# A two-layer hybrid encoder: pair rows of 288 columns, operands at multiples of 256 bytes

## The chip, the core and the metric

The kernel runs on one core of one Trainium2 chip. The metric is the device time of one execution in microseconds. A core has TensorE (PE, the matrix engine, with a sequence of weight loads, PEld, beside the matmuls), VectorE (DVE), ScalarE (ACT), GpSimd (POOL) and SyncE (SP, which here issues the transfers from the main memory HBM). Data lies in SBUF, 128 partitions with a byte address within the partition; TensorE writes its sums to PSUM, 8 banks of 512 float32 per partition. All engines run beside each other and wait for each other by semaphores.

## The reference, cut to what matters

Two layers of an encoder over 16 meta tokens and 256 tokens (272 in all) of width 2048:

```python
for l in range(2):
    proj = h @ w_in[l]                      # 2048 -> 6176 columns
    gq, gk, gv, gr, glr, nq, nk, nv = split(proj)
    y_gla = gated_linear_attention(gq, gk, gv, gr, glr)    # both directions
    y_na = neighbourhood_attention(nq, nk, nv)
    mix = concat(y_gla, y_na) @ w_out[l]    # 2048 -> 2048
    h = layer_norm(ALPHA * h + mix)
    ff = square(relu(h @ w_ff1[l])) @ w_ff2[l]             # 2048 -> 8192 -> 2048
    h = layer_norm(ALPHA * h + ff)
return h[:, 16:]
```

All of it is float32. The weights of the four dense products are some 400 MB; each is read once.

## The kernel before, in words

**Float32 from pairs.** A float32 matmul is made of faster ones on a reduced type (`F32R`). Every operand is split into a high part, the value rounded to `F32R`, and a low part, the value minus the high part (`split`, L262: a ScalarE copy for the high part and a VectorE subtraction for the low one). A product is then high times high, high times low and low times high.

**Pairs of activations.** The activations are held transposed: a *pair* (L41, made by `pair`, L272) holds 128 of the 2048 columns, one per partition, and in each partition two rows: the high part of all tokens and, behind it, the low part. There are 16 x pairs (the normed input of a layer or of its MLP), 16 y pairs (the concatenated attention outputs, later the first 16 chunks of the MLP's inner activations), and for the MLP 16 u pairs more (its other inner chunks; L786). An x pair's rows are 274 float32 wide, because two more columns hold a layer norm's gain and bias; y and u rows are 272 wide. The sums over partitions that the layer norms and the GLA heads need (`mean`, L871, matmuls at L878) go through pairs named `sp`. Pools place tiles one behind the other, each rounded up to 32 bytes; constants come first (L74), then x pairs (pool `xhl`), y pairs (`yhl`), and the weight tiles (`wst`).

**Weight tiles.** `order` (L145) yields all weights in the order of their use in tiles of 128 partitions x 1024 float32. `made` (L167) loads a tile to `raw` by SyncE's queue, copies it to `wh` on ScalarE (L175) and makes `wl` on VectorE (L176). Each of the three names has three buffers; two tiles are kept ready ahead of TensorE (L161).

**The dense products.** `by_m` (L245) makes 128 output columns at a time: for each weight tile, `eight` (L199) multiplies 8 chunks of 128 x 128 weights with 8 pairs. In layer 0, with 272 tokens, L211 does 16 matmuls of 272 columns per tile (`wh` chunk j with the high row, then with the low row of pair j) and L214 does 8 (`wl` chunk j with the high row). In layer 1 only the 256 tokens count (`once`): L208 does 8 matmuls of 512 columns, which read 256 columns of the high row and 256 of the low row of a pair in one instruction, and L214 does 8 of 256 columns. Where a product needs the gain and bias columns too, there are 274 or 258 columns. `by_k` (L225, matmuls at L241) runs over the input chunks in the outer loop, where the input becomes ready chunk by chunk; its matmuls have the same operands.

**Order of the work.** TensorE's queue is strict: tiles of dense products, and between them, by credits (`pump`, L116), steps of generators for the GLA heads, the neighbourhood attention and the layer norms. The order is fixed when the program is built. Names in the profile: `mm<-x,wh` is a matmul with a moving row of an x pair and a stationary chunk of `wh`.

Other tiles take the places of pairs that are not in use: `load_gates` (L369) puts gate weights in y pairs, `reuse` (L936) puts output rows and the last layer norm's rows in x pairs; both take 512 columns of the two rows seen as one.

Of the kernel before, what the change touches and what calls it, by code (L numbers as in the profile page):

```python
# [7 lines left out]
F32 = mybir.dt.float32  # L8
F32R = mybir.dt.float32r
# [5 lines left out]
P = 128  # L15
# [4 lines left out]
L = T + NM  # L20
# [15 lines left out]
LEAD = 4  # L36
WARM = 14
MEET = 2


class Pair(tuple):  # L41
# [8 lines left out]
class Trunk:  # L50
# [23 lines left out]
    def consts(self):  # L74
        nc, c = self.nc, self.cp
        t = lambda n, s, d=F32: c.tile(s, d, name=n, tag=n)
        self.vec = t("vec", [P, DEPTH, 66])
        nc.sync.dma_start(self.vec, self.i["vec"].rearrange("l p v -> p l v"))
        self.ident = t("ident", [P, P])
        nc.sync.dma_start(self.ident, self.i["ident"])  # L80
        self.sel = t("sel", [LRK, 2])
        nc.sync.dma_start(self.sel, self.i["sel"])
        self.qmask = t("qmask", [NM, NK2])
        nc.sync.dma_start(self.qmask, self.i["qmask"])
        self.mask = t("mask", [P, 5, 32], U8)
        raw = self.wp.tile([P, WB], F32, name="raw", tag="raw")[:, :5 * 32].rearrange("p (l c) -> p l c", l=5)
        nc.sync.dma_start(raw, self.i["mask"])
        nc.gpsimd.tensor_copy(self.mask, raw)
        self.ones = {}
        for n in (GDV, 4 * P, D):  # L90
            self.ones[n] = t(f"ones{n}", [P, P])
            nc.gpsimd.memset(self.ones[n], 1.0 / n)
        self.ones_r = {}
        for n in self.ones:
            self.ones_r[n] = t(f"onesr{n}", [P, P], F32R)
            nc.scalar.copy(self.ones_r[n], self.ones[n])
        self.eps = t("eps", [P, 1])
        nc.gpsimd.memset(self.eps, EPS)
        self.one = t("one", [P, 1])
        nc.gpsimd.memset(self.one, 1.0)  # L100
# [15 lines left out]
    def pump(self, fg, bg, meet=False):  # L116
# [10 lines left out]
        while self.credit >= 1:  # L127
            if self.bg and self.wants.get(self.bg[0]):
                alone = meet and not some
                if ran or alone and self.late < MEET:  # L130
                    self.late += alone and not ran
# [138 lines left out]
        self.nc.vector.tensor_tensor(dst[low:low + n], src, dst[high[0]:high[0] + n].bitcast(F32), ALU.subtract)  # L270

    def pair(self, pool, name, c):  # L272
        w = L + 2 if name == "x" else L
        return Pair(pool.tile([P, 2, w], F32R, name=f"{name}{c}", tag=f"{name}{c}", bufs=1))


    def layer(self, l):
# [90 lines left out]

    def load_gates(self):  # L369

        place = lambda c: self.yp.tile([P, 2, L], F32, name=f"gw{c}", tag=f"y{c}", bufs=1).rearrange("p a c -> p (a c)")[:, :512]
        *self.wup, self.wlr = (place(c) for c in (8, 9, 10))
        for d, w in enumerate(self.wup):
            self.nc.sync.dma_start(w[:LRK], self.i["wup"][self.l, :, d])
        self.nc.sync.dma_start(self.wlr, self.i["wlr"][self.l])
# [559 lines left out]

    def reuse(self, name, c, dtype):  # L936

        t = self.xp.tile([P, 2, L + 2], dtype, name=f"{name}{c}", tag=f"x{c}", bufs=1)
        return t.rearrange("p a c -> p (a c)")[:, :512]

    def affine(self, l, which, k):
# [231 lines left out]
```

## Time and profile before

| what | value |
|---|---|
| time, median of 3 runs | 2379.57 us (2379.57 to 2380.83) |
| span of the profiled execution, first to last instruction | 2377.1 us |
| mean granted TensorE clock | 0.999 |
| instructions in the profile | 44606 |
| HBM read, mean rate | 414.03 MB, 175 GB/s |

The profile gives the span of its execution; the time of a run is taken outside the core and is longer by what lies around the span, here 2.5 us between the median and the profiled span.

How to read it. The page has numbered parts: busy time of each engine; the span in 40 slices; the DMA queues; the chain of work that ended last, followed back from the last instruction; groups of instructions; transfers. A group's row reads: line, engine, operation, output<-inputs by the program's names, shape, count, then busy us and mean ns of one, then idle time before them. Matmuls are pipelined, so the mean of one (some 290 ns) is far longer than the distance from one to the next. In the timeline, equal instructions in a row are merged: start in us, length in us, engine, line, operation, count. The distance between the starts of two such rows is the time that the engine took from the one to the other.

### The profile page before, as it was taken

The numbers are of one execution on the slowest core, as the hardware profiler recorded it, in microseconds if no ns is written. First come the engines' busy times: TensorE is split into PE (matmuls) and PEld (weight loads), VectorE is DVE, ScalarE is ACT, GpSimd is POOL, SyncE is SP. The second block draws the span as 40 slices with busy tenths as digits, with TensorE's granted clock in tenths as the row PEclk, the third lists the DMA queues.
The fourth block names the chain that finished last, engine by engine and source line by source line (L and its number), as shares of the span: only waits on it lengthen the run. The fifth ranks groups of instructions, "written<-read, shape, count | busy, mean of one in ns | idle before, by whom it ended". The sixth has DMA issues, their size and how long they took to land.

```text
span 2377.1 us, 44606 instructions
## 1 busy us (share of the span) xinstructions
PE 2368.7 (100%) x18180; PEld 2249.8 (95%) x18180; DVE 1520.7 (64%) x2432; ACT 1221.2 (51%) x2100; POOL 135.2 (6%) x200
## 2 busy tenths in 40 slices
PE   9999999999999999999999999999999999999998
PEld 9999999999999999999999899999988888888888
DVE  5588777775544455546576787778766455666654
ACT  5666664564433344444456667655644333444443
POOL 0011100100000000000021111000100000000000
PEclk9999999999999999999999999999999999999999
DMA  8455445555555555565555555556666666666664
GB/s 261 152 159 152 148 138 171 174 173 175 177 177 177 174 175 178 171 176 176 175 186 163 168 164 154 161 154 192 193 189 186 187 189 190 188 187 206 199 192 143
DMA packets 118301, 419.02 MB, mean 176 GB/s; under 512 B 13512, under 2 KB 14024, under 8 KB 118096
## 3 DMA queue, kind: packets, MB, share of 16 engines
q1 hardware_dynamic: 117808, 415.65, 57.9%
q8 instruction: 142, 2.33, 0.4%
q14 instruction: 63, 0.52, 0.1%
q10 hardware_dynamic: 288, 0.52, 0.1%
HBM read 414.03 MB, written 2.10 MB: 175 GB/s over the span
## 4 chain that ended last, share of the span: by engine, by line
PE 98%; DVE 1%; issue 0%; ACT 0%; POOL 0%; DVEq 0%; ACTq 0%; POOLq 0%
PE mm L211 36%; PE mm L214 29%; PE mm L208 22%; PE mm L241 6%; PE bg L241 1%; PE bg L752 1%; PE mm L691 1%; PE bg L552 0%; PE bg L398 0%; DVE wl L176 0%; PE mm L717 0%; PE mm L441 0%; PE bg L878 0%; PE bg L603 0%; PE bg L633 0%
## 5 line engine op out<-in xcount | busy, mean ns | idle before, releaser
L176 DVE TENSOR_TENSOR wl<-raw,wh 128x1024 fp32r<-128x1024 f32 (+1 forms) x768 | 941.5, 1227 | 633.7 <-ACT wh L175 625.0
L175 ACT CAST wh<-raw 128x1024 fp32r<-128x1024 f32 (+1 forms) x768 | 804.1, 1048 | 932.7 <-PE mm L211 432.6
L211 PE MATMUL mm<-x,wh 128*128 128x272 f32 (+2 forms) x4224 | 577.8, 289 | 0.0
L211 PEld LDWEIGHTS mm<-x,wh 128*128 128x128 f32 x4224 | 548.5, 189 | 0.8 <-PE mm L691 0.2
L214 PE MATMUL mm<-x,wl 128*128 128x272 f32 (+3 forms) x3264 | 467.3, 285 | 0.0
L214 PEld LDWEIGHTS mm<-x,wl 128*128 128x128 f32 x3264 | 437.6, 188 | 13.2
L208 PE MATMUL mm<-x,wh 128*128 128x512 f32 x1152 | 293.7, 397 | 0.0
L208 PEld LDWEIGHTS mm<-x,wh 128*128 128x128 f32 x1152 | 207.7, 189 | 39.4 <-PE mm L691 0.4
L214 PE MATMUL mm<-y,wl 128*128 128x272 f32 (+1 forms) x1408 | 199.0, 284 | 0.0
L211 PE MATMUL mm<-y,wh 128*128 128x272 f32 (+1 forms) x1440 | 195.2, 287 | 0.0
L214 PEld LDWEIGHTS mm<-y,wl 128*128 128x128 f32 x1408 | 188.1, 188 | 7.4
L211 PEld LDWEIGHTS mm<-y,wh 128*128 128x128 f32 x1440 | 185.9, 188 | 0.0
L208 PE MATMUL mm<-y,wh 128*128 128x512 f32 x688 | 172.6, 392 | 0.0
L214 PE MATMUL mm<-u,wl 128*128 128x272 f32 (+1 forms) x1024 | 144.5, 283 | 0.0
L208 PEld LDWEIGHTS mm<-y,wh 128*128 128x128 f32 x688 | 123.1, 188 | 21.2
L211 PE MATMUL mm<-u,wh 128*128 128x272 f32 (+1 forms) x1056 | 142.6, 287 | 0.0
L214 PEld LDWEIGHTS mm<-u,wl 128*128 128x128 f32 x1024 | 136.6, 188 | 5.6
L211 PEld LDWEIGHTS mm<-u,wh 128*128 128x128 f32 x1056 | 135.9, 188 | 0.0
L208 PE MATMUL mm<-u,wh 128*128 128x512 f32 x496 | 125.3, 395 | 0.0
L208 PEld LDWEIGHTS mm<-u,wh 128*128 128x128 f32 x496 | 89.1, 188 | 16.4
L241 PE MATMUL mm<-x,wh 128*128 128x272 f32 (+1 forms) x512 | 73.1, 287 | 0.0
L241 PEld LDWEIGHTS mm<-x,wh 128*128 128x128 f32 x512 | 67.5, 189 | 0.0
(273 smaller groups left out, 1853.6 us busy)
## 6 DMA issues: line engine op xcount, KB each, us to landing
raw<-in_wff SPq DMA_DIRECT2D x512, 512.0 KB, 3.6
raw<-in_win SPq DMA_DIRECT2D x190, 512.0 KB, 4.0
raw<-in_wout SPq DMA_DIRECT2D x64, 512.0 KB, 3.7
nb<-in_nab SPq DMA_DIRECT2D x16, 352.0 KB, 4.8
xraw<-in_xT SPq DMA_DIRECT2D x7, 272.0 KB, 6.3
out<-out SPq DMA_DIRECT2D x5, 256.0 KB, 3.2
brow<-in_norm SPq DMA_DIRECT2D x4, 256.0 KB, 5.5
gw<-in_wup SPq DMA_DIRECT2D x4, 196.0 KB
```

The costliest lines, as they stand in the source:

```text
L175: nc.scalar.copy(wh[:, c], raw[:, c])
L176: self.wl = nc.vector.tensor_tensor(wl[:, c], raw[:, c], wh[:, c].bitcast(F32), ALU.subtract).ins
L208: mm(ps, lhsT=c(wh, j), rhs=v.both[:, :, :T], start=first and not j, stop=False)
L211: mm(ps[:, :n], lhsT=c(wh, j), rhs=v[i][:, :n], start=first and not i + j, stop=False)
L214: mm(o, lhsT=c(wl, j), rhs=h[:, :T if once else n], start=False, stop=last and j == 7)
L241: self.nc.tensor.matmul(ps[g + m][:, :n], lhsT=parts[p][0][:, c:c + P], rhs=acts[k + j][parts[p][1]][:, :n], start=k + j + p == 0, stop=k ...
L691: nc.tensor.matmul(ps[hh][:, t * NKEY:t * NKEY + NKEY], lhsT=q[hs, NM + t * P:NM + t * P + P], rhs=k[hs, t, :], start=True, stop=True)
L752: nc.tensor.matmul(po[t][hs, :P], lhsT=v2[ts, hs] if rest else v1[:, t, hs], rhs=p2[ts, hh, :] if rest else p1[:, 2 * hh + t, :], start=re ...
```

## The change

Rows of every pair become 288 float32 wide (1,152 bytes), so that a pair takes 2,304 bytes, nine times 256. A tile of 40 float32 per partition, which nothing reads or writes, goes ahead of the constants and moves all that follows. By the built program's addresses, x pairs then begin at byte 13,056, y pairs at 49,920, `raw`, `wh` and `wl` at 86,784, 99,072 and 111,360, u pairs at 124,672, all at multiples of 256; a pair's low row begins 1,152 bytes behind its high row. Before, x pairs began at byte 21,088 and stood 2,208 bytes apart, y pairs began at 56,416 and u pairs at 129,120, both 2,176 apart, and the weight tiles began at 91,232, 103,520 and 115,808. The wider rows take more space; the constructor's reserve for software-made DMA descriptors at the start of SBUF is halved from 16,384 to 8,192 bytes. The places that reuse pairs follow the new width. What the instructions read, compute and write is the same.

```diff
+PAD = 40
+PITCH = 288
...
     def consts(self):
         nc, c = self.nc, self.cp
         t = lambda n, s, d=F32: c.tile(s, d, name=n, tag=n)
+        t("pad", [P, PAD])
         self.vec = t("vec", [P, DEPTH, 66])
...
     def pair(self, pool, name, c):
-        w = L + 2 if name == "x" else L
-        return Pair(pool.tile([P, 2, w], F32R, name=f"{name}{c}", tag=f"{name}{c}", bufs=1))
+        return Pair(pool.tile([P, 2, PITCH], F32R, name=f"{name}{c}", tag=f"{name}{c}", bufs=1))
...
     def load_gates(self):
-        place = lambda c: self.yp.tile([P, 2, L], F32, name=f"gw{c}", tag=f"y{c}", bufs=1).rearrange("p a c -> p (a c)")[:, :512]
+        place = lambda c: self.yp.tile([P, 2, PITCH], F32, name=f"gw{c}", tag=f"y{c}", bufs=1).rearrange("p a c -> p (a c)")[:, :512]
...
     def reuse(self, name, c, dtype):
-        t = self.xp.tile([P, 2, L + 2], dtype, name=f"{name}{c}", tag=f"x{c}", bufs=1)
+        t = self.xp.tile([P, 2, PITCH], dtype, name=f"{name}{c}", tag=f"x{c}", bufs=1)
...
-    nc = bacc.Bacc("TRN2", target_bir_lowering=False, num_devices=1)
+    nc = bacc.Bacc("TRN2", target_bir_lowering=False, num_devices=1, dynamic_dma_scratch_size=8192)
```

## The prediction

> **What bounds the kernel now.** I read the page's parts 1, 3 and 4 first, to see which engine sets the end.
>
> ```profile
> PE 2368.7 (100%) x18180; PEld 2249.8 (95%) x18180; DVE 1520.7 (64%) x2432; ACT 1221.2 (51%) x2100; POOL 135.2 (6%) x200
> ...
> q1 hardware_dynamic: 117808, 415.65, 57.9%
> ...
> PE 98%; DVE 1%; issue 0%; ACT 0%; POOL 0%; DVEq 0%; ACTq 0%; POOLq 0%
> PE mm L211 36%; PE mm L214 29%; PE mm L208 22%; PE mm L241 6%; PE bg L241 1%; PE bg L752 1%; PE mm L691 1%; PE bg L552 0%; PE bg L398 0%; DVE wl L176 0%; PE mm L717 0%; PE mm L441 0%; PE bg L878 0%; PE bg L603 0%; PE bg L633 0%
> ```
>
> TensorE is busy for the whole span and makes up 98% of the chain that ended last; 93% of the chain are the four lines of the dense matmuls (L211, L214, L208, L241). Transfers take 57.9% of the DMA engines, VectorE is at 64%: neither is late for anything. So the change is worth what it does to the time of one matmul, times some 16,000.
>
> That time is best read from the timeline of TensorE, where the matmuls of one weight tile stand as one row and the distance of two starts is the time of a whole tile. Before the change, in layer 0, on the x pairs (start us, us, line, operation):
>
> ```profile
> 603.64 2.18 PE L211 MATMUL mm<-x,wh 128*128 128x272 f32 x16
> ...
> 606.66 2.18 PE L211 MATMUL mm<-x,wh 128*128 128x272 f32 x16
> ...
> 609.69 2.18 PE L211 MATMUL mm<-x,wh 128*128 128x272 f32 x16
> ```
>
> Two tiles of 24 matmuls (16 of L211, 8 of L214) take 609.69 - 603.64 = 6.05 us: 3.025 each, 126 ns per matmul. The same view on the y and u pairs, whose matmuls have the same shape and count:
>
> ```profile
> 798.51 2.18 PE L211 MATMUL mm<-y,wh 128*128 128x272 f32 x16
> ...
> 801.52 2.15 PE L211 MATMUL mm<-y,wh 128*128 128x272 f32 x16
> ...
> 804.50 2.16 PE L211 MATMUL mm<-u,wh 128*128 128x272 f32 x16
> ...
> 807.49 2.16 PE L211 MATMUL mm<-u,wh 128*128 128x272 f32 x16
> ...
> 810.47 2.18 PE L211 MATMUL mm<-y,wh 128*128 128x272 f32 x16
> ```
>
> 3.01, 2.98, 2.99 and 2.98 us, on average 11.96 / 4 = 2.99. Nothing but the place of the operands in the memory differs between these tiles and the x tiles, so **place does cost something**: 0.035 us per tile (1.2%) between x and y or u, and 0.03 between two halves of y. In layer 1, where L208 reads both rows of a pair in one matmul of 512 columns:
>
> ```profile
> 1271.99 2.03 PE L208 MATMUL mm<-x,wh 128*128 128x512 f32 x8
> ...
> 1274.80 2.03 PE L208 MATMUL mm<-x,wh 128*128 128x512 f32 x8
> ...
> 1277.60 0.54 PE L398 MATMUL bg<-x,ws 128*64 128x272 f32 x3
> ```
>
> ```profile
> 1960.08 2.00 PE L208 MATMUL mm<-y,wh 128*128 128x512 f32 x8
> ...
> 1962.85 2.01 PE L208 MATMUL mm<-y,wh 128*128 128x512 f32 x8
> ...
> 1965.64 2.02 PE L208 MATMUL mm<-u,wh 128*128 128x512 f32 x8
> ...
> 1968.45 2.02 PE L208 MATMUL mm<-u,wh 128*128 128x512 f32 x8
> ```
>
> x takes 5.61 / 2 = 2.805 us per tile, y 2.77 and 2.79, u 2.81: (1968.45 - 1960.08) / 3 = 2.79 on average.
>
> What part of a tile could a better place save? The last tiles of the program have the shape of layer 0 with 256 columns:
>
> ```profile
> 2358.19 2.05 PE L211 MATMUL mm<-u,wh 128*128 128x256 f32 x16
> ...
> 2361.02 2.05 PE L211 MATMUL mm<-u,wh 128*128 128x256 f32 x16
> ```
>
> 2.83 us against u's 2.985 with 272 columns: 16 columns cost 0.155 us / 24 = 6.5 ns, 0.40 ns a column. At that rate 272 columns are 110 ns, and some 15 of the 125 ns of a matmul do not grow with its columns. Only those can go.
>
> **The change part by part.** *Instructions.* None is added or removed. On TensorE, ScalarE, VectorE and SyncE the built programs have the same instructions in the same order with the same waits; one semaphore signal at the end of layer 0's last L214 tiles comes one matmul earlier, because a memset of GpSimd then overlaps u28 where it overlapped u29. No wait is new, nothing is queued behind anything else. The smaller scratch in the constructor is reserved memory for descriptors that no transfer of this kernel uses (the queues of part 3 are hardware queues): 0.
>
> *Addresses.* The tiles' sizes and the pools' order give them, and the built program lists them. Before, x pairs stand 2,208 bytes apart from byte 21,088 on and their low row begins 1,096 bytes after the high one: high rows begin at a multiple of 64 for odd chunks and 32 past one for even chunks, low rows 8 past a multiple of 32. y and u pairs stand 2,176 bytes apart, both rows always 32 past a multiple of 64. Weight tiles begin 96 past a multiple of 256. After, every high row and every weight tile begins at a multiple of 256, every low row 128 past one.
>
> *What that does to x.* The x tiles are the only ones with rows of several kinds of start, and they take longest in layer 0. After the change they have one kind, as y and u have had. The nearest price is y's and u's own level: x goes from 3.025 to 2.99. The number of such tiles, from the groups by form:
>
> ```profile
> L211 PE MATMUL mm<-x,wh 128*128 128x272 f32 x3584 | 491.1, 289 | 0.0
> L208 PE MATMUL mm<-x,wh 128*128 128x512 f32 x1152 | 293.7, 397 | 0.0
> ...
> L211 PE MATMUL mm<-y,wh 128*128 128x272 f32 x1408 | 191.2, 287 | 0.0
> L208 PE MATMUL mm<-y,wh 128*128 128x512 f32 x688 | 172.6, 392 | 0.0
> ...
> L211 PE MATMUL mm<-u,wh 128*128 128x272 f32 x1024 | 138.5, 287 | 0.0
> L208 PE MATMUL mm<-u,wh 128*128 128x512 f32 x496 | 125.3, 395 | 0.0
> ```
>
> 3584 / 16 = 224 tiles: -224 x 0.035 = **-7.8 us**. In layer 1, 1152 / 8 = 144 tiles from 2.805 to 2.79: -144 x 0.015 = **-2.2 us**. Other forms on x, of 274 and 258 columns and by L241:
>
> ```profile
> L211 PE MATMUL mm<-x,wh 128*128 128x272 f32 (+2 forms) x4224 | 577.8, 289 | 0.0
> ...
> L241 PE MATMUL mm<-x,wh 128*128 128x272 f32 (+1 forms) x512 | 73.1, 287 | 0.0
> ```
>
> are (4224 - 3584) / 16 + 512 / 16 = 72 tiles, at the same 0.035: **-2.5 us**.
>
> [...]
>
> *What that does to y and u.* They had one kind of start (32 past a multiple of 64) and get another. The bounds come from their own spread, 2.98 to 3.01, and x's 3.025; their mean is the value I take: 0. The 88 + 64 tiles of layer 0 may move by -0.01 to +0.035 each (-1.5 to +5.3 us), the 86 + 62 of layer 1 from -0.02 to +0.015 (-3.0 to +2.2).
>
> *Is a start at a multiple of 64 worth more in itself?* The trace has one place where rows begin there one after the other: the sums of the layer norms (L878) in layer 1, on the sp pairs; in layer 0 the same matmuls begin 32 past such a multiple.
>
> ```profile
> 1650.10 0.52 PE L878 MATMUL bg<-sp,onesr 128*128 128x256 f32 x3
> 1650.46 0.52 PE L211 MATMUL mm<-x,wh 128*128 128x258 f32 x3
> ```
>
> ```profile
> 454.38 0.66 PE L878 MATMUL bg<-sp,onesr 128*128 128x272 f32 x4
> 454.88 0.29 PE L211 MATMUL mm<-x,wh 128*128 128x274 f32 x1
> ```
>
> 0.36 / 3 = 120 ns with 256 columns aligned, 0.50 / 4 = 125 with 272 not aligned; less 16 columns of 0.40 that is 118.5. Aligned rows are no faster there. That their weights stood 32 past a multiple of 64 is what this does not answer.
>
> *Transfers, copies, splits.* Weight rows now land at a multiple of 256, and ScalarE and VectorE read and write other addresses: 57.9%, 51% and 64% busy beside a full TensorE, so even 10% more or less on them would not reach the end. What hides them is TensorE's own work; without that cover a change of 10% on VectorE, the busier of the two, would be some 150 us of its 1520.7.
>
> *Sum.* -7.8 - 2.2 - 2.5 = -12.5 us on a span of 2377.1, so 2364.6. The runs' median is 2379.57, 2.5 us over the profiled span, and I add those: **2367 us**.
>
> **The rivals.**
>
> *Place makes no difference on the whole* (chance 0.20): a long or a short tile is a matter of which row meets which weight chunk, and a new layout reshuffles them with the same mean. For it: y's halves, with equal kinds of rows, differ by 0.03. Time: 2379.6, within 4.8 us.
>
> *Collision, slower* (chance 0.30): rows and weight chunks begin in the same class of addresses after the change, in each of the matmuls, where before only some did. If TensorE's two streams, moving rows and the next weights, get in each other's way when they start in the same class, each tile pays what now only some pay. For it: x against y, and y's halves, show that pairing has a price. Against it: the sp rows, and that y's even rows start in the weights' class (96 past a multiple of 256) without standing out as a whole tile. Price: y and u go to x's level, 152 x 0.035 + 148 x 0.015 = +7.5 us; if x too goes up by one more such step, (152 + 224 + 72) x 0.035 + 144 x 0.015 = +17.8 more. 2387 to 2405, I take 2392. It decides as soon as a tile in layer 0 takes over 3.02 on average. [...]
>
> *A whole block is saved per row* (chance 0.12): if rows are fetched in blocks of 64 bytes, a row that begins 32 past a multiple touches one block more than an aligned one, 16 columns or 6.5 ns. For it: 15 ns per matmul don't grow with the columns, and no trace here has aligned rows together with aligned weights. Against it: the sp rows, and x, whose odd high rows are aligned already (8 of a tile's 24 rows) and which is no faster. Price: y and u 24 rows, x 16 rows: (152 + 148) x 24 x 6.5 ns = 47 us, (224 + 144 + 72) x 16 x 6.5 ns = 46 us; 93 in all, 2287. [...]
>
> **How the numbers follow.** The forecast has a chance of 0.38 (own range 2355 to 2374), no difference 0.20, collision 0.30, the block 0.12. A measurement of this kernel can tell 0.2% (4.8 us) from no change. Faster: 0.38 + 0.12 = 0.50; same 0.20; slower 0.30. The range leaves out the block and the upper part of collision: 2348 to 2402.
>
> **What would show it.** Right: in the timeline of layer 0, x tiles every 2.99 us, as y and u, and these where they were; in layer 1 about 2.79 for all. Slower tiles of all three names would show collision; tiles near 2.85 (layer 0) and 2.65 (layer 1) the block. The count of instructions, the granted clock and the share of the chain must stay; were TensorE to wait for weights, or DVE and ACT forms to change by over 10%, the argument that only TensorE matters would be wrong.

## The result and the profile after

| | before | after |
|---|---|---|
| time, median of 4 runs each | 2379.67 us (2379.57 to 2380.83) | 2369.47 us (2368.6 to 2370.26) |
| span of the profiled execution | 2377.1 us | 2367.7 us |

The ratio is 0.9957, with a 95% interval from 0.9945 to 0.9969: 10.2 us faster, 2.5 us above the forecast of 2367.

Parts 1, 3 and 4 of the page after. All line numbers of the dense products are three higher than before: L214 was L211, L217 was L214, L211 was L208, L244 was L241.

```profile
PE 2359.4 (100%) x18180; PEld 2241.3 (95%) x18180; DVE 1520.6 (64%) x2432; ACT 1220.3 (52%) x2100; POOL 136.0 (6%) x200
...
q1 hardware_dynamic: 117808, 415.65, 57.7%
...
PE 98%; DVE 1%; issue 0%; ACT 0%; POOL 0%; DVEq 0%; ACTq 0%; POOLq 0%
```

TensorE's busy time fell by 9.3 us (2368.7 to 2359.4) and the span by 9.4; counts, VectorE, ScalarE and the transfers' share are what they were. So the whole difference lies in how long the same matmuls take. The timeline of TensorE in layer 0, the same tiles as in the prediction, first x, then y and u:

```profile
601.63 2.14 PE L214 MATMUL mm<-x,wh 128*128 128x272 f32 x16
...
604.61 2.14 PE L214 MATMUL mm<-x,wh 128*128 128x272 f32 x16
```

```profile
792.35 2.14 PE L214 MATMUL mm<-y,wh 128*128 128x272 f32 x16
...
795.33 2.14 PE L214 MATMUL mm<-y,wh 128*128 128x272 f32 x16
...
798.31 2.14 PE L214 MATMUL mm<-u,wh 128*128 128x272 f32 x16
...
801.29 2.14 PE L214 MATMUL mm<-u,wh 128*128 128x272 f32 x16
...
804.27 2.14 PE L214 MATMUL mm<-y,wh 128*128 128x272 f32 x16
```

Every tile takes 2.98 us now, whichever pair it reads; before, x took 3.025 and y and u between 2.98 and 3.01. In layer 1:

```profile
1261.87 2.02 PE L211 MATMUL mm<-x,wh 128*128 128x512 f32 x8
...
1264.68 2.02 PE L211 MATMUL mm<-x,wh 128*128 128x512 f32 x8
...
1267.48 4.15 PE L400 MATMUL bg<-x,ws 128*64 128x272 f32 x32
```

```profile
1949.88 2.02 PE L211 MATMUL mm<-y,wh 128*128 128x512 f32 x8
...
1952.69 2.02 PE L211 MATMUL mm<-y,wh 128*128 128x512 f32 x8
...
1955.50 2.02 PE L211 MATMUL mm<-u,wh 128*128 128x512 f32 x8
```

All take 2.81 (5.61 / 2 and 5.62 / 2): x as before, y longer (before 2.77 and 2.79).

**Where the time came from** is seen by laying the same tile of both traces side by side. The x tile of layer 0 that started at 606.66 starts at 601.63, 5.03 us ahead; the x tile of 512 columns at 1271.99, early in layer 1, at 1261.87, 10.12 ahead. The lead still grows, to some 11.8 us near 1563, while x tiles of 272 columns run in layer 1 too; then it shrinks: the y tile at 1960.08 starts at 1949.88, 10.20 ahead, and the last u tiles at 2358.19 start at 2348.86, 9.33 ahead:

```profile
2348.86 2.06 PE L214 MATMUL mm<-u,wh 128*128 128x256 f32 x16
...
2351.72 2.06 PE L214 MATMUL mm<-u,wh 128*128 128x256 f32 x16
```

The gain is made on tiles of 272 columns, most of them in layer 0, and some 2.5 us of it are given back in the rest of layer 1.

In these two traces a tile's time mostly repeats to a few ns over the tiles of one kind that stand behind the same set, so below it is given in ns, as the median distance from a tile's first matmul to the next tile's. Sets are the 8 pairs that one weight tile meets: x0-7, x8-15, y0-7, y8-15, u16-23, u24-31. From here on "layer 0" stands for tiles of 272 columns and "layer 1" for those of 512. By the built program, 40 of the 224 x tiles of 272 columns run in layer 1, where keys and values are made for all tokens.

| set (tiles in layer 0, layer 1) | before: layer 0, layer 1 | after |
|---|---|---|
| x0-7, x8-15 (224, 144) | 3027, 2807 | 2980, 2807 |
| y0-7 (44, 43) | 3011, 2776 | 2980, 2807 |
| y8-15 (42, 41) | 2975, 2791 | 2980, 2807 |
| u16-31 (64, 62) | 2987, 2807 | 2980, 2807 |

224 x -0.047 = -10.5 us on x in layer 0; y and u in layer 0 -1.4 + 0.2 - 0.4 = -1.6; y in layer 1 +1.3 + 0.7 = +2.0. That makes -10.1 us for a span that is 9.4 shorter. The 0.7 between them are `by_k`'s matmuls (L241): summed over the starts of all matmuls of both traces, they take some 0.7 us longer after the change.

### The profile page after: what moved, and what is told of

The parts are those of the page before. It is cut to its first block, busy times and chain, and to the rows that moved or that the text cites. A ratio compares the mean times of both kernels' runs of the same rounds, so it can differ in the third digit from the quotient of the medians.

```text
span 2367.7 us, 44607 instructions
## 1 busy us (share of the span) xinstructions
PE 2359.4 (100%) x18180; PEld 2241.3 (95%) x18180; DVE 1520.6 (64%) x2432; ACT 1220.3 (52%) x2100; POOL 136.0 (6%) x200
## 4 chain that ended last, share of the span: by engine, by line
PE 98%; DVE 1%; issue 0%; ACT 0%; POOL 0%; DVEq 0%; ACTq 0%; POOLq 0%
PE mm L214 35%; PE mm L217 29%; PE mm L211 22%; PE mm L244 6%; PE bg L244 1%; PE bg L754 1%; PE mm L693 1%; PE bg L554 0%; PE bg L400 0%; DVE wl L179 0%; PE mm L719 0%; PE mm L443 0%; PE bg L880 0%; PE bg L605 0%; PE bg L635 0%
## 5 line engine op out<-in xcount | busy, mean ns | idle before, releaser
L214 PE MATMUL mm<-x,wh 128*128 128x272 f32 (+2 forms) x4224 | 569.7, 287 | 0.0
L214 PEld LDWEIGHTS mm<-x,wh 128*128 128x128 f32 x4224 | 541.0, 188 | 0.8 <-PE mm L693 0.2
L217 PE MATMUL mm<-x,wl 128*128 128x272 f32 (+3 forms) x3264 | 466.3, 285 | 0.0
L217 PEld LDWEIGHTS mm<-x,wl 128*128 128x128 f32 x3264 | 436.9, 188 | 12.7
L211 PE MATMUL mm<-x,wh 128*128 128x512 f32 x1152 | 292.1, 396 | 0.0
L211 PEld LDWEIGHTS mm<-x,wh 128*128 128x128 f32 x1152 | 207.5, 189 | 38.4 <-PE mm L693 0.4
L217 PE MATMUL mm<-y,wl 128*128 128x272 f32 (+1 forms) x1408 | 200.0, 284 | 0.0
L217 PEld LDWEIGHTS mm<-y,wl 128*128 128x128 f32 x1408 | 189.0, 188 | 7.4
L214 PE MATMUL mm<-y,wh 128*128 128x272 f32 (+1 forms) x1440 | 193.3, 286 | 0.0
L214 PEld LDWEIGHTS mm<-y,wh 128*128 128x128 f32 x1440 | 184.3, 188 | 0.0
L211 PE MATMUL mm<-y,wh 128*128 128x512 f32 x688 | 174.3, 395 | 0.0
L217 PE MATMUL mm<-u,wl 128*128 128x272 f32 (+1 forms) x1024 | 145.4, 284 | 0.0
L211 PEld LDWEIGHTS mm<-y,wh 128*128 128x128 f32 x688 | 123.9, 189 | 22.4
L217 PEld LDWEIGHTS mm<-u,wl 128*128 128x128 f32 x1024 | 137.5, 188 | 5.4
L214 PE MATMUL mm<-u,wh 128*128 128x272 f32 (+1 forms) x1056 | 141.2, 286 | 0.0
L214 PEld LDWEIGHTS mm<-u,wh 128*128 128x128 f32 x1056 | 134.8, 188 | 0.0
L211 PE MATMUL mm<-u,wh 128*128 128x512 f32 x496 | 125.4, 395 | 0.0
L211 PEld LDWEIGHTS mm<-u,wh 128*128 128x128 f32 x496 | 89.4, 189 | 16.3
L244 PE MATMUL mm<-x,wh 128*128 128x272 f32 (+1 forms) x512 | 73.5, 289 | 0.0
L244 PEld LDWEIGHTS mm<-x,wh 128*128 128x128 f32 x512 | 68.0, 191 | 0.0
```

The costliest lines, as they stand in the source:

```text
L211: mm(ps, lhsT=c(wh, j), rhs=v.both[:, :, :T], start=first and not j, stop=False)
L214: mm(ps[:, :n], lhsT=c(wh, j), rhs=v[i][:, :n], start=first and not i + j, stop=False)
L217: mm(o, lhsT=c(wl, j), rhs=h[:, :T if once else n], start=False, stop=last and j == 7)
L244: self.nc.tensor.matmul(ps[g + m][:, :n], lhsT=parts[p][0][:, c:c + P], rhs=acts[k + j][parts[p][1]][:, :n], start=k + j + p == 0, stop=k ...
```

## The experiments

The theories: **mixed starts** (the prediction's): a tile whose rows have several kinds of start takes longer, one with one kind takes y's level. **Low rows**: only x's low rows, 8 past a multiple of 16 bytes, cost. **Aligned**: a start at a multiple of 64 or 256 is worth something in itself. **Pairing**: what counts is how far a row lies from the weight chunk that it meets, not where either begins. That distance, the row's first byte less the weight chunk's, is given modulo 256 unless the text says otherwise. Beside each kernel ran the kernel before on the same chip. All but `e12` are single runs. The nine runs of the kernel before beside `e12` lie between 2379.37 and 2382.23 us, so a difference of 2 or 3 us between single times is no more than noise unless the tile times say the same. Those repeat to a few ns in long stretches of one kind, and e2 and e3, on which most rests, have one time in all sets.

### The change's parts: x alone, y and u alone

`e1_x_alone` is the kernel before, x rows widened and nothing else (the smaller scratch makes room):

```diff
-        w = L + 2 if name == "x" else L
+        w = 288 if name == "x" else L
...
-        t = self.xp.tile([P, 2, L + 2], dtype, name=f"{name}{c}", tag=f"x{c}", bufs=1)
+        t = self.xp.tile([P, 2, 288], dtype, name=f"{name}{c}", tag=f"x{c}", bufs=1)
...
```

> The kernel before, with x rows 288 wide and nothing else: x pairs stand 2,304 bytes apart and begin in the weights' class (96 past a multiple of 256); y, u and the weights keep the classes that they had. Tiles in layer 0 by the timeline: if x took long because its low rows begin 8 past a multiple of 16 (theory 'low rows') or because its pairs begin now at a multiple of 64 and now 32 past one (theory 'mixed starts'), x goes from 3.027 to 2.98 us, y and u stay at 3.01, 2.975 and 2.987, and layer 1 stays as before (x 2.807, y 2.776 and 2.791). The span is then 2377.1 - 10.4 = 2366.7. If multiples of 256 in themselves count (theory 'aligned'), x stays at 3.027 and the span at 2377.

2368.22 us beside 2379.23. Timeline of x and of y in layer 0 (lines as before):

```profile
601.23 2.14 PE L211 MATMUL mm<-x,wh 128*128 128x272 f32 x16
...
604.21 2.14 PE L211 MATMUL mm<-x,wh 128*128 128x272 f32 x16
```

```profile
792.51 2.18 PE L211 MATMUL mm<-y,wh 128*128 128x272 f32 x16
...
795.52 2.15 PE L211 MATMUL mm<-y,wh 128*128 128x272 f32 x16
...
798.50 2.16 PE L211 MATMUL mm<-u,wh 128*128 128x272 f32 x16
```

x takes 2.98 as after, y and u their old 3.01 and 2.98. Here x rows and weights begin 96 past a multiple of 256, so no row or weight stands at a multiple of 256: the width of the x rows alone gives all of the gain.

`e10_y_u_alone` widens the others instead:

```diff
-        w = L + 2 if name == "x" else L
+        w = L + 2 if name == "x" else 288
...
```

> The kernel before with only the y and u rows 288 wide, x rows 274 as they were. If the parts add up, x stays at 3.027 and 2.807 us per tile and y and u go to the changed kernel's 2.980 and 2.807: y0-7 44 x -0.031 + 43 x +0.031, y8-15 42 x +0.005 + 41 x +0.016, u 64 x -0.007, together about +0.4 us, so 2379.5 to 2380.5. If the parts do not add up (each needs the other, as when a tile's first matmuls depend on the tile before), the time leaves that by over 2 us.

2379.94 us beside 2379.80. x stays at 3027 and 2807 ns, y and u go to 2980 and 2807. The parts add up, and the y and u part is worth nothing on the whole.

### Is it the place itself?

`e2_all_32_on` moves everything 32 bytes further; `e3_weights_32_on` moves the weight tiles alone by 32 bytes, while rows stay at multiples of 256.

```diff
-PAD = 40
+PAD = 48
```

```diff
         self.jp = pool("jn", bufs=1)
+        self.wp.tile([P, 8], F32, name="wpad", tag="wpad", bufs=1)
+        self.jp.tile([P, 56], F32, name="jpad", tag="jpad", bufs=1)
```

> The changed kernel with 32 bytes more ahead of the constants: every pair row and every weight tile keeps its place relative to the others and begins 32 bytes past a multiple of 128. 'Low rows', 'mixed starts' and 'pairing' (what counts is where a row begins relative to the weight chunk) all expect the changed kernel's 2.980 us in layer 0 and 2.807 in layer 1 for all tiles, span 2367.7. 'Aligned' expects a loss of what the change gained: about 3.02 in layer 0, span near 2377.

> The changed kernel with the weight tiles alone 32 bytes further on; pairs still begin at multiples of 256. 'Pairing' expects other tile times than 2.980 and 2.807, by some 0.01 to 0.05 us per tile in either direction, the same for x, y and u. 'Low rows' and 'mixed starts' expect 2.980 and 2.807 unchanged, span 2367.7. 'Aligned' expects a loss in all tiles.

e2: 2369.77 us, 2980 and 2807 ns in every set, as the changed kernel (lines as after):

```profile
601.66 2.14 PE L214 MATMUL mm<-x,wh 128*128 128x272 f32 x16
...
604.64 2.14 PE L214 MATMUL mm<-x,wh 128*128 128x272 f32 x16
...
607.62 2.14 PE L214 MATMUL mm<-x,wh 128*128 128x272 f32 x16
```

e3: 2382.26, beside 2379.23 for the kernel before on that chip. Its timeline (two lines were added above, so L216 is the changed kernel's L214, L213 its L211):

```profile
604.96 2.17 PE L216 MATMUL mm<-x,wh 128*128 128x272 f32 x16
...
607.96 2.17 PE L216 MATMUL mm<-x,wh 128*128 128x272 f32 x16
...
610.97 2.17 PE L216 MATMUL mm<-x,wh 128*128 128x272 f32 x16
```

```profile
1961.00 2.03 PE L213 MATMUL mm<-y,wh 128*128 128x512 f32 x8
...
1963.82 2.03 PE L213 MATMUL mm<-y,wh 128*128 128x512 f32 x8
```

3.007 and 2.82 us, in all sets. "Aligned" falls twice: without alignment nothing is lost (e2), and with rows still at multiples of 256 the gain is gone and more (e3). The weights begin 32 past a multiple of 256 in both, so their own place is not it either. What e3 changed is the distance between rows and weights, by 32 bytes: **pairing**.

### Where in the pair the low row stands, and the step from pair to pair

`e4_low_rows` keeps each pair at its place and changes the low row's distance from the high one, by set:

```diff
+        pitch = {"x": (274, 276), "y": (280, 284), "u": (286, 282)}.get(name, (288, 288))[c // 8 % 2]
+        t = pool.tile([P, 2 * PITCH], F32R, name=f"{name}{c}", tag=f"{name}{c}", bufs=1)
+        return Pair(t[:, :2 * pitch].rearrange("p (a c) -> p a c", a=2))
```

> The changed kernel, each pair still 2,304 bytes from the next and its high row at a multiple of 256, but the low row begins elsewhere: 1,096 bytes behind the high row in x0 to x7 (8 past a multiple of 16, as before the change), 1,104 in x8 to x15, 1,120 in y0 to y7, 1,136 in y8 to y15, 1,144 in u16 to u23 and 1,128 in u24 to u31 (the last two again 8 past a multiple of 16). 'Low rows' expects about 3.02 us per tile in layer 0 for x0 to x7 and both sets of u, 2.98 for the three others. 'Mixed starts' expects 2.980 for all six. 'Pairing' expects six different values between 2.97 and 3.06 that do not go by multiples of 16.

2383.89 us beside 2379.23. Low row 1096 bytes behind (x0-7): 3009 and 2827 ns; 1104 (x8-15): 3025, 2800; 1120: 3015, 2805; 1128: 3018, 2807; 1136: 2999, 2824; 1144: 3013, 2804; and 1152, as in the changed kernel: 2980, 2807. Timeline of x, first tile x0-7, second x8-15:

```profile
606.60 2.17 PE L214 MATMUL mm<-x,wh 128*128 128x272 f32 x16
...
609.61 2.18 PE L214 MATMUL mm<-x,wh 128*128 128x272 f32 x16
...
612.63 2.17 PE L214 MATMUL mm<-x,wh 128*128 128x272 f32 x16
```

Every set here has one kind of high and one kind of low row, yet 1104 takes as long as x before: **mixed starts falls**. e3 says so too, and there all sets have one and the same layout: one kind of start, and 3007 ns. 1096, 1128 and 1144, 8 past a multiple of 16, do not stand out, 1104, a multiple of 16, is the longest in layer 0: low rows falls.

`e6_steps` keeps the low row at 1152 and changes the step between pairs (x0-7 2272 bytes, x8-15 2432, y 2240, u16-23 2560, u24-31 2368; the changed kernel has 2304):

```diff
+        n = {"x": (568, 608), "y": (560, 560), "u": (640, 592)}.get(tag, (576, 576))[c // 8 % 2]
+        return pool.tile([P, n], dtype, name=f"{name}{c}", tag=f"{tag}{c}", bufs=1)
...
```

> The changed kernel with its rows' place in the pair kept (low row 1152 behind the high one) and only the step from pair to pair changed: x0-7 2272 bytes, x8-15 2432, all y 2240, u16-23 2560, u24-31 2368, where the changed kernel has 2304. By 'the distance from row to weight chunk counts, within 256 bytes' u16-23 (2560, always distance 0) stay at 2.980 and 2.807 us; x8-15 (distances 0 and 128 in turn, so high and low row in turn in the weights' class) near 2.98 to 2.99; x0-7, y and u24-31, whose distances run through multiples of 32 or 64, 2.99 to 3.03 like x before (3.027). By 'a longer period than 256 counts' u16-23 leave 2.980 although their distance within 256 is the same. By 'only the low row's place in the pair counts' (rival) all sets stay at 2.980 and 2.807. Whole: 2372 to 2385 us by the first, 2369.5 by the last.

2378.37 us beside 2379.72. Layer 0, in the order of the sets: 3011, 3003, 3012, 3003, 2996, 3002; x8-15's 3003 is over the expected 2.98 to 2.99. u16-23 in layer 1:

```profile
1963.96 2.04 PE L211 MATMUL mm<-u,wh 128*128 128x512 f32 x8
...
1966.79 2.03 PE L211 MATMUL mm<-u,wh 128*128 128x512 f32 x8
```

2.83 us, although each high row stands at a multiple of 256 from its chunk and each low row 128 past one, as in the changed kernel. Chunks are 512 bytes apart; with 2304 the high rows' distances are 0 and 256 in turn modulo 512, with 2560 always 0. So either a distance counts within more than 256 bytes, or another set in the tile ahead makes the difference (in e9 below, the tile ahead does). `e7_before_weights_512_on`, the kernel before with weights (and u) 512 bytes further, asks after how many bytes a distance repeats:

```diff
+        t("pad", [P, 2048])
...
+        self.wp.tile([P, 128], F32, name="wpad", tag="wpad", bufs=1)
...
```

> The kernel before, with weight tiles, and u pairs behind them, 512 bytes further; x and y pairs stay. It asks why y8-15 (2.975 us in layer 0, 2.791 in layer 1) and u (2.987 and 2.807) differ in the kernel before although their rows stand to the weight chunks alike within 512 bytes. By 'distance within 256 or 512 counts' nothing moves: y0-7 3.011 and 2.776, y8-15 2.975 and 2.791, u 2.987 and 2.807, x 3.027 and 2.807, whole 2379.5. By 'distance within 1024 or more counts' y0-7 and y8-15 change (y8-15 to u's 2.987 and 2.807 if it is 1024) and u stays. By 'absolute places count' (rival: y lies in another part of the memory than u) y stays as it was.

2379.46 us beside 2379.72, and the median of every set is where it was to 1 ns. For these layouts a shift by 512 is no shift. One stretch differs all the same. In the attention's output product tiles of y0-7 and y8-15 alternate. First the kernel before, then e7 (its L213 is L211 there), both beginning with a tile of y8-15:

```profile
397.41 2.15 PE L211 MATMUL mm<-y,wh 128*128 128x272 f32 x16
...
400.38 2.18 PE L211 MATMUL mm<-y,wh 128*128 128x272 f32 x16
...
403.40 2.15 PE L211 MATMUL mm<-y,wh 128*128 128x272 f32 x16
```

```profile
397.66 2.18 PE L213 MATMUL mm<-y,wh 128*128 128x272 f32 x16
...
400.69 2.17 PE L213 MATMUL mm<-y,wh 128*128 128x272 f32 x16
...
403.69 2.18 PE L213 MATMUL mm<-y,wh 128*128 128x272 f32 x16
```

y8-15 and y0-7 take 2975 and 3012 ns in the kernel before, 3028 and 2999 in e7, tile after tile through the stretch. e1 has the kernel before's y rows at the same distances without the shift, and takes 3028 and 2999 there too. So **one layout can run in two courses**, and each repeats itself until other work comes between.

So another 512 is not why y8-15 (2975) differ from u (2987) at equal distances modulo 512. The likely reason is again what ran ahead: by the starts of single matmuls only the first six of a y8-15 tile are shorter than u's, and what stands ahead of them is y0-7 at other distances. The built program does not lay the y pairs in the order of their numbers: y0 begins at byte 71,648 and y8 at 65,120. Against the weights at 103,520, y0-7 so stand 128 further, modulo 256, than y8-15 and u, which is why y's halves could take 3011 and 2975 with the same kinds of start.

### How fine, and is any distance good?

`e5_row_offsets`, `e8_offsets_by_16` and `e11_offsets_by_4` move both rows of a pair together against the weights, each set by its own amount, with pads between the pools and a first column `on` in the pair (shown for e11):

```diff
-        return Pair(pool.tile([P, 2, PITCH], F32R, name=f"{name}{c}", tag=f"{name}{c}", bufs=1))
+        on = {"x": (2, 6), "y": (3, 5), "u": (4, 1)}.get(name, (0, 0))[c // 8 % 2]
+        return Pair(pool.tile([P, 2, PITCH], F32R, name=f"{name}{c}", tag=f"{name}{c}", bufs=1)[:, :, on:])
...
```

> The changed kernel, with both rows of a pair moved together against the weight tiles: x0-7 begin 32 bytes past the weights' place within 256, x8-15 64, y0-7 96, y8-15 128, u16-23 160, u24-31 192. Spacing and low row (+1152) stay. Known so far per tile (layer 0, layer 1): distance 0 gives 2.980 and 2.807 us, distance -32 (weights moved on by 32) 3.007 and 2.820. 'Pairing by the distance from row to weight chunk': each set takes a time of its own between about 2.97 and 3.03 us; 128 (high and low row change places) comes near 2.980 again. Two levels ('multiples of 64 are good'): 64, 128 and 192 give 2.98, 32, 96 and 160 give 3.007. 'The rows' own place' (the weights' place is nothing): all sets as their absolute starts say, x0-7 as the kernel with everything 32 bytes on, 2.980; that theory has no answer to the 3.007 measured already. Whole: 2370 to 2385 us by pairing.

> The changed kernel with both rows of a pair moved against the weight tiles by x0-7 16 bytes, x8-15 48, y0-7 112, y8-15 144, u16-23 176, u24-31 208. Measured before, layer 0 and layer 1: 0 gives 2.980 and 2.807 us, 32 2.993 and 2.804, 64 3.021 and 2.796, 96 3.017 and 2.815, 128 2.983 and 2.808, 160 2.985 and 2.794, 192 3.015 and 2.804, 224 3.007 and 2.820. By 'the distance acts smoothly' the new ones lie between their neighbours: 16 at 2.987, 48 at 3.007, 112 at 3.000, 144 at 2.984, 176 at 3.000, 208 at 3.011 within 0.008. By 'a grain of 32 bytes or more' each is equal to the neighbour below or above it. By 'a grain finer than 32' they are times of their own, outside the neighbours. Whole by the first: 2375.5, within 2.

> The changed kernel with both rows of a pair a few bytes past the weights' place: x0-7 8, x8-15 24, y0-7 12, y8-15 20, u16-23 16, u24-31 4. Measured per tile, layer 0 and layer 1: 0 gives 2.980 and 2.807 us, 16 (x0-7) 2.984 and 2.744, 32 2.993 and 2.804. u16-23 asks whether 16 repeats on other pairs: 2.984 and 2.744 if the distance is what counts, something else if it was x's tile before it. By 'steps of 16 bytes count' 4, 8 and 12 are equal to 0 (2.980 and 2.807), or to 16, and 20 and 24 to 16. [...] By 'every byte of distance counts' they are times of their own, between 2.97 and 3.03, and in layer 1 between 2.74 and 2.83. Whole: 2362 to 2378.

2376.16 us (beside 2379.72), 2363.57 (2379.80) and 2391.46 (2380.23). The last two lie outside what was expected of the whole (2375.5 within 2, and 2362 to 2378). Tile times in ns by distance in bytes:

| distance | layer 0 | layer 1 | | distance | layer 0 | layer 1 |
|---|---|---|---|---|---|---|
| 0 (after) | 2980 | 2807 | | 64 | 3021 | 2796 |
| 4 | 3078 | 2870 | | 96 | 3017 | 2815 |
| 8 | 3043 | 2801 | | 112 | 2991 | 2783 |
| 12 | 2979 | 2792 | | 128 | 2983 | 2808 |
| 16 (x0-7, e8) | 2984 | 2744 | | 144 | 2972 | 2801 |
| 16 (u16-23, e11) | 2987 | 2771 | | 160 | 2985 | 2794 |
| 20 | 3062 | 2887 | | 176 | 2987 | 2814 |
| 24 | 2991 | 2859 | | 192 | 3015 | 2804 |
| 32 | 2993 | 2804 | | 208 | 3018 | 2809 |
| 48 | 2989 | 2783 | | 224 (e3) | 3007 | 2820 |
| 16 (all sets, e12, below) | 2980 | 2817, 2796 | | | | |

Read the table with care: but for 0, 224 and the last row, each set stood behind a set at another distance, and what ran ahead counts too. In e11's own trace y0-7 take 2979 ns in layer 0 behind u24-31 and 2962 behind y8-15; in e5's, y8-15 take 3010 in the attention's output product and 2983 in the MLP, behind y0-7 both times. In layer 1 one distance, 16, gives 2744 to 2817, so that column is no curve of the distance. In layer 0 the distances of 4, 8 and 20 (3043 to 3078) lie further from 2980 than the 53 ns by which one layout was seen to differ with its course (2975 and 3028, above). There a few bytes count, and neither a grain nor a smooth curve shows: 12 and 16 are good, 8 and 20 between and beside them bad. "Multiples of 64 are good" falls (64 and 192 take 3021 and 3015, 160 takes 2985), and 12, no multiple of 16, is as short as 0 (2979 and 2980). The worst kernel of the study, e11, has rows of the changed kernel's width; y and u in its layer 0 (distances 12, 20, 16, 4 in turn):

```profile
799.94 2.15 PE L214 MATMUL mm<-y,wh 128*128 128x272 f32 x16
...
802.92 2.20 PE L214 MATMUL mm<-y,wh 128*128 128x272 f32 x16
...
805.99 2.15 PE L214 MATMUL mm<-u,wh 128*128 128x272 f32 x16
...
808.97 2.21 PE L214 MATMUL mm<-u,wh 128*128 128x272 f32 x16
...
812.05 2.15 PE L214 MATMUL mm<-y,wh 128*128 128x272 f32 x16
```

2.98, 3.07, 2.98, 3.08. And the best single time is e8's. Its x in layer 1, 16 and 48 in turn (L213 is the changed kernel's L211, L219 its L217):

```profile
2019.51 2.00 PE L213 MATMUL mm<-x,wh 128*128 128x512 f32 x8
2021.35 1.07 PE L219 MATMUL mm<-x,wl 128*128 128x256 f32 x8
2022.26 2.00 PE L213 MATMUL mm<-x,wh 128*128 128x512 f32 x8
2024.10 1.10 PE L219 MATMUL mm<-x,wl 128*128 128x256 f32 x8
2025.04 2.00 PE L213 MATMUL mm<-x,wh 128*128 128x512 f32 x8
```

2.75 and 2.78 us: at distance 16 the 8 matmuls with `wl` take 0.91 us (2022.26 - 2021.35) where they take 0.94 at 48 (2025.04 - 2024.10).

### Rows and weights in one class

`e9_low_rows_further` tries the collision rival of the prediction at its strongest: x0-7 with step 2560 and the low row 1280 behind, so that both rows always begin in the weights' class modulo 256. y has step 2432 and low rows at 1216, u16-23 low rows at 1088, u24-31 at 1148.

```diff
+        t, low = self.room(pool, F32R, name, c), {"x": (320, 288), "y": (304, 304), "u": (272, 287)}.get(name, (288, 288))[c // 8 % 2]
+        return Pair(bass.AP(t.tensor, t.offset, [t.ap[0], [low, 2], [1, L + 2 if name == "x" else L]]))
...
```

> The changed kernel with other places of the low row, all high rows at multiples of 256 as the weights. x0-7: step 2560, low row 1280 behind, so that both rows always begin in the weights' class within 256. x8-15 as in the changed kernel (control). y: step 2432, low row +1216. u16-23: step 2304, low +1088 (as u before). u24-31: low +1148, no multiple of 16. By 'rows and weights in one class collide' (a rival of the prediction) x0-7 go well over 3.02 us in layer 0 and over 2.82 in layer 1. By 'pairing, each layout a draw' x0-7 come between 2.97 and 3.03 as the other layouts did, with no special place for equal classes. [...] Controls x8-15: 2.980 and 2.807, but for the first matmuls after x0-7. Whole 2370 to 2384 by pairing, over 2390 by the first.

2378.31 us beside 2379.80. In layer 0, first a tile of x0-7, then one of x8-15:

```profile
604.73 2.17 PE L214 MATMUL mm<-x,wh 128*128 128x272 f32 x16
...
607.74 2.16 PE L214 MATMUL mm<-x,wh 128*128 128x272 f32 x16
...
610.73 1.54 PE L214 MATMUL mm<-x,wh 128*128 128x272 f32 x11
```

By the medians x0-7 take 3013 and 2793 ns. In layer 0 that is longer than the changed kernel's 2980, but y (3017 and 3015) and u16-23 (3012), whose low rows are not in the weights' class, take as long, and in layer 1 x0-7 are shorter than the changed kernel's: equal classes are a layout among others, not a collision. u24-31 with 1148, no multiple of 16, take 2989. The control missed: x8-15, laid out as in the changed kernel, take 2998 in layer 0 for 2980. Ahead of each stood a tile of x0-7 with another layout, so **the tile ahead counts too**, and not for the first matmuls alone: the first 16 matmuls of an x8-15 tile come every 124 to 128 ns, where in the changed kernel most of them come every 121 and 126 in turn.

### All rows 16 bytes past the weights

`e12_rows_16_on` takes the best distance of layer 1 for all sets:

```diff
-        return Pair(pool.tile([P, 2, PITCH], F32R, name=f"{name}{c}", tag=f"{name}{c}", bufs=1))
+        on = 4 if name in "xyu" else 0
+        return Pair(pool.tile([P, 2, PITCH], F32R, name=f"{name}{c}", tag=f"{name}{c}", bufs=1)[:, :, on:])
...
```

> The changed kernel with both rows of all x, y and u pairs 16 bytes past the weights' place. If the distance alone counts, every set repeats what x0-7 gave at 16: 2.984 us in layer 0 and 2.744 in layer 1, where the changed kernel has 2.980 and 2.807. 292 tiles of layer 1 x -0.063 = -18.4, 376 of layer 0 x +0.004 = +1.5, so 2369.5 - 16.9 = 2352.6. If the tile before counts too, as u16-23 at 16 hint (2.987 and 2.771 behind tiles at another distance), 292 x -0.036 + 376 x 0.007 = -7.9: 2361.6. If the gain in layer 1 was an accident of the alternation of 16 and 48 on x, 2.80 again and 2369 to 2371. The rows begin at 16 past a multiple of 256, so if a start at a multiple of 32 or 64 were worth anything in itself, it would be slower than the changed kernel.

2366.14 us (2365.58 to 2366.33, 5 runs) beside 2380.31; ratio 0.9939, 95% interval 0.9926 to 0.9953. None of the three expectations came as a whole: the tiles are those of the last, the time lies below it. Layer 0 takes 2980 ns in every set, as in the changed kernel. In layer 1:

```profile
1946.75 2.03 PE L211 MATMUL mm<-y,wh 128*128 128x512 f32 x8
...
1949.57 2.01 PE L211 MATMUL mm<-y,wh 128*128 128x512 f32 x8
...
1952.36 2.03 PE L211 MATMUL mm<-u,wh 128*128 128x512 f32 x8
```

2.82 and 2.79 in turn, from one and the same layout, where x0-7 of e8 at this distance took 2.744. In the attention's output product it is the other way round: there y0-7 take 2796 and y8-15 2817. So a tile's time isn't a function of its own distances: what ran ahead of it settles which course it takes. By the starts of all matmuls of both traces, the 3.2 us by which the span (2364.5) is below the changed kernel's are small parts: 1.2 from the 24 tiles of 274 columns (3000 ns for 3047), 0.8 from layer 1's tiles, 0.7 from `by_k` and 0.6 from layer 0's. This version beats the kernel before; that it beats the changed kernel (its interval reaches into that one's 0.9945 to 0.9969) is likely but was not measured side by side.

## Why the prediction was right, point by point

**TensorE alone bounds the kernel: held.** Busy time and span fell alike (9.3 and 9.4 us).

**x in layer 0, -7.8 us: the right step with the wrong reason and a size too small.** x went from 3.027 to 2.980 us, -10.5. It was to come to y's and u's mean of 2.99 because its rows would have one kind of start. e4 has sets with one kind of start at 3.025, e3 has the changed kernel's rows at 3.007: uniform rows are not enough. x had drawn a poor layout, and the new one's 2980 is, by luck, among the shortest of some forty that were run (2972 to 3078 in layer 0). The forecast's own sentence for the rival "no difference", that a tile's time is a matter of which row meets which chunk, names the cause; what it got wrong is that the mean would stay.

**x in layer 1, -2.2, and its other forms, -2.5: did not come.** x takes 2807 ns in layer 1 as before; tiles of 274 columns went from 3060 to 3047 ns, those of 258 from 2887 to some 2905, 24 and 15 of them: -0.3 and +0.3 us; those of L241 on x take 0.5 us more in sum. These 4.7 us are more than the error of the whole, and the larger gain of x in layer 0 made up for 2.7 of them. That the total came within 2.5 us is luck, then: errors of both signs, and a mechanism that is not the one forecast.

**y and u, 0: held in sum** (-1.6 in layer 0, +2.0 in layer 1; e10 +0.1 on the whole), but not tile by tile: y0-7 went down by 31 ns in layer 0 and up by 31 in layer 1, where the bounds allowed 10 down and 15 up. The sums stayed near the bounds (-1.5 and +2.2) because these parts have both signs.

**The rivals.** No difference: the time left its 4.8 us. Its evidence, y's halves, were not alike as the prediction took them to be: they stand 128 bytes apart against the weights (e7). It is y8-15's even high rows and y0-7's odd ones that begin in the weights' class, not all even ones. Collision: not from equal classes (e9's x0-7), but its kind of price is real: e3's 2382.26 us and e11's 2391.46 are this kernel at worse distances, and e11's lies where that rival put its time (2387 to 2405). Moving the weights alone by 32 bytes against the rows cost 12.5 us (2382.26 of e3 - 2369.77 of e2). A whole block per row: no set of layer 0 came near 2.85 us (2972 to 3078 ns).

**Open.** That the distance from row to chunk counts (e2 against e3), that a few bytes of it matter (e11), that a shift of 512 bytes changed no set's median in the kernel before (e7), and that what ran ahead acts on a tile (e9, e11, e12, and the two courses of one layout in e7 and the kernel before) is shown. How much of a set's time is its distance and how much its course is not shown where the sets of a kernel differ, nor is what every single step of 4 bytes does. Whether and where the two streams meet, whether it is the chunk in use or the next one being loaded, and why some tiles settle at 121 and 126 ns a matmul in turn (after) and others at 132 and 121 (x8-15 of e5), is open. A search over layouts was not made.

## What to carry to other kernels

When TensorE is all of the chain, read the distance between two weight tiles' starts for each operand: if equal matmuls differ by a per cent between tensors (here tiles of 3027 and 2987 ns on x and u), their places are worth a look. Do not expect alignment as such to help (e1 and e2, with no row or weight tile at a multiple of 256, took 2368.22 and 2369.77 us, the changed kernel 2369.47): change one tensor's row width or one pad at a time, and measure, for rows of the same width gave 2363.57 to 2391.46 us with offsets of 4 to 208 bytes. Measure the whole kernel and not one tensor alone, since a tile's time also hung on what ran ahead of it (x8-15 in the changed kernel's layout took 2998 ns in e9 for 2980). A layout that wins in one shape need not win in another: the change took y0-7 from 3011 to 2980 ns with 272 columns and from 2776 to 2807 with 512.

## What was not expected of the hardware

- Moving the weights by 32 bytes against the rows made the tiles of every set longer, 2980 to 3007 ns; moving rows and weights together by 32 made none longer (e3, e2).
- Rows 4 bytes past the weights' place took 3078 ns a tile, 12 bytes past it 2979 (e11): 4 ns for each matmul. One layout alone was seen to differ by 53 with its course.
- With 256 columns, matmuls settled at 113 ns in x0-7 of e8 and at about 118 in the changed kernel.
- The same layout alternated between 2817 and 2796 ns from tile to tile (e12), and took 2998 for 2980 when the tile ahead of it had another layout (e9).
- The same y rows and weights, in the same stretch of work, took 3012 and 2975 ns in turn in one run (before) and 2999 and 3028 in two others (e1, e7).
